# Gate and up projections of a hybrid decoder trunk by seven block products, with the feed-forward units in two parts

## The chip, the cores and the metric

The kernel runs on one core of a Trainium2 chip. The metric is the device time of one launch in microseconds (us). A core has a matrix engine (TensorE, PE in the rows; PEld is its weight load), VectorE (DVE), ScalarE (ACT), GpSimd (POOL) and a queue that issues the DMAs (SP). Each works through its own queue in order and waits for the others by semaphores. SBUF is the working memory, PSUM holds the matrix products in eight banks of 512 float32 a partition.

## The reference

Two layers over 512 tokens of width 1024. Each has a mixer of three sorts of attention heads, a SwiGLU feed-forward of 2816 units, and a gated layer embedding. The change touches the feed-forward alone:

```
h = h + o @ w_out[i]
hn = rms_norm(h, norm_ffn[i])
h = h + (silu(hn @ w_ffn_gate[i]) * (hn @ w_ffn_up[i])) @ w_ffn_down[i]
gate = sigmoid(rms_norm(h, norm_ple[i]) @ w_ple_gate[i])
h = h + (p[i] @ w_ple_proj[i]) * gate
```

All of it is float32 at the interface.

## The kernel before

Every projection is made of three matmuls (`mm3`, L221): both operands are split into a high half, rounded to the matrix engine's float32 format, and a low half, the rest; high x high, high x low and low x high are summed in PSUM. So a weight tile has a path: a DMA into `wraw` (`load_raw`, L192; three buffers of 128x1024, each the rows of four row tiles by 256 columns), ACT copies 512 columns of it into the high half of `whl` (L198), POOL or DVE subtracts that from the raw weights into the low half (L201), and PE loads both halves as weights. `lo_turn` says which of the two: in the feed-forward it is 2, every second low half goes to POOL. There are five `whl` buffers.

`feed_forward` (L1120) first normalizes the rows and transposes them (`norm_T`, L372) into `xT`: activations with the model width on the partitions, in high and low halves, four tiles. Then it goes through 11 blocks of 256 units. Per block, gate and then up: four `whl` tiles each, every tile for 12 matmuls of 512 tokens. A PSUM bank holds 128 units x 512 tokens; a block takes two for gate and two for up. When a block is done, ACT computes Silu from PSUM, DVE multiplies it by up from PSUM, ACT and POOL make the high and low half of `hid`. Block 0 goes first over tokens 0 to 255 and then over the rest, since the later tokens are normalized last. When all 11 blocks are done, the down projection runs over all 22 tiles of units, once for output columns 0 to 511 and once for 512 to 1023, and DVE adds the sums to `h` (L1025).

The order of each engine's queue is set when the program is built, from priorities in the code (`prio`, and `issue_after` for a few) and from what depends on what. `utile` buffers (15 of 128x2048) hold `xT`, `hid`, gains and other large tiles.

Of the kernel before, what the change touches and what calls it, by code (L numbers as in the profile page):

```python
# [10 lines left out]
F32 = mybir.dt.float32  # L11
# [8 lines left out]
P = 128  # L20
S = 512
# [21 lines left out]
def hybrid_trunk_kernel(  # L43
# [47 lines left out]
    def etile(name="e"):  # L91
        return upool.tile([P, 512], F32, name=name, tag="e", bufs=4)
# [97 lines left out]
    turn, lo_turn = [0], [3]  # L190

    def load_raw(view, k, c):  # L192
        raw = wpool.tile([P, 1024], F32, name="wraw", tag="wraw", bufs=3)
        nc.sync.dma_start(raw[:, :k * c].rearrange("p (k c) -> p k c", k=k), view)
        return raw

# [175 lines left out]
    def norm_T():  # L372
# [746 lines left out]

    def feed_forward(i, add_h, between):  # L1120
        lo_turn[0] = 2
        xact = norm_T()
        hidden = []
        for fp in range(NF // 2):
            hid = utile([P, 2, 2, S], name="hid")
            hidden.append(hid)
            tags = "ddss" if fp % 2 == 0 else "stto"
            accs = [bank(t, name=f"gu{j}") for j, t in enumerate(tags)]

            def part(w, a2, ks, cols):  # L1130
                for k, (hi, lo) in ks:
                    for j in range(2):
                        cs = slice(j * P, (j + 1) * P)
                        m = mm3(a2[j][:, cols], hi[:, cs], lo[:, cs], xact(k, 0)[:, cols], xact(k, 1)[:, cols],
                                k == 0 and cols.start == 0, k == KD - 1)
                        if k == 0 and cols.start == 0:
                            first.append(m.ins)

            for wi, w in enumerate((w_ffn_gate[i], w_ffn_up[i])):
                ws = enumerate(weights(w, allk, fp * 256, 256, 2))  # L1140
                first = []
                if fp == 0:

                    ws = list(ws)
                    part(w, accs[2 * wi:2 * wi + 2], ws, slice(0, 256))
                    with tc.issue_after(first[1]):
                        part(w, accs[2 * wi:2 * wi + 2], ws, slice(256, 512))
                else:
                    part(w, accs[2 * wi:2 * wi + 2], ws, slice(0, 512))
            for j in range(2):  # L1150
                sg = etile("sg")
                se.activation(sg, accs[j], AF.Silu)
                ve.tensor_tensor(sg, sg, accs[2 + j], op=ALU.mult)
                se.activation(hid[:, 0, j, :], sg, AF.Copy)
                ge.tensor_tensor(hid[:, 1, j, :], sg, f(hid[:, 0, j, :]), op=ALU.subtract)

        def hact(k, half, tt):
            return hidden[k // 2][:, half, k % 2, tt * P:(tt + 1) * P]

        for c, tags in ((0, "ddss"), (512, "stto")):  # L1160
            if c:
                between()
            else:
                load_gain(norm_ple[i])
            run(project(hact, w_ffn_down[i], list(range(NF)), c, 512, add_h(c), tags=tags, tail=2 if c == 0 else 4))


    def layer_embedding(i):
# [164 lines left out]
```

## Time and profile before

| | |
|---|---|
| median of 3 runs | 1575.32 us (1571.79 to 1575.82) |
| the profiled execution | 1575.22 us, its span 1573.5 us |
| PE busy | 1516.4 us, 96% |
| DVE busy | 746.1 us, 47% |
| ACT busy | 733.1 us, 47% |
| POOL busy | 577.4 us, 37% |
| gate and up, matmuls of 512 columns | 3 x 640, 251 us for each 640 |
| gate and up, matmuls of 256 columns (block 0) | 3 x 128, 36 us for each 128 |

Busy times of one engine can be set side by side along the time axis. Matmuls overlap, so their mean duration is longer than the step from one start to the next; where PE's pace matters, the starts are read. A row of a group gives a mean over the whole kernel, in which undisturbed operations and held ones are mixed; a row of the timeline gives one operation, or several alike in a row (x2) with their time from the first start to the last end.

### The profile page before, as it was taken

Reading aid. Unit: us, or ns where it says so; the run is one execution under the profiler, and the core shown is the slowest. Engines: PE = TensorE matmul, PEld = TensorE weight load, DVE = VectorE, ACT = ScalarE, POOL = GpSimd, SP = SyncE. Lnnn points to the kernel's source line nnn. Section 1 sums busy time; section 2 is a strip of 40 time slices with the busy share of each in tenths; the row PEclk is TensorE's granted clock in tenths of the full one; section 3 lists DMA queues with packets and bytes.
Section 4 is the critical chain, followed back from the end, with each engine's and each line's share of the span. In section 5 each row is a group of like instructions: output and inputs, shape, how many; then the busy total and the mean of one; then the engine's idle time right before and its main releaser. Section 6 shows DMA issues by size and latency. Waiting matters only on the chain.

```text
span 1573.5 us, 23178 instructions
## 1 busy us (share of the span) xinstructions
PE 1516.4 (96%) x8626; PEld 1286.3 (82%) x8626; DVE 746.1 (47%) x1588; ACT 733.1 (47%) x1561; POOL 577.4 (37%) x636
## 2 busy tenths in 40 slices
PE   6999999999999999999999999999999999999997
PEld 6898877879888888888988988778788888888887
DVE  7777869763211111214386878796621111112153
ACT  5467667654333332323355767686433333323243
POOL 4323545453333333321233235465333333323223
PEclk9999999999999999999999999999999999999999
DMA  5411321122333323321224121212133323333221
GB/s 163 136 56 42 82 68 34 48 95 70 97 102 94 94 94 121 119 96 67 81 72 126 49 71 52 80 33 75 55 103 98 94 94 94 100 114 121 94 70 65
DMA packets 114449, 134.58 MB, mean 86 GB/s; under 512 B 6864, under 2 KB 91936, under 8 KB 114336
## 3 DMA queue, kind: packets, MB, share of 16 engines
q1 hardware_dynamic: 114336, 133.10, 27.5%
q8 instruction: 68, 1.11, 0.3%
q14 instruction: 45, 0.37, 0.1%
HBM read 122.59 MB, written 2.10 MB: 79 GB/s over the span
## 4 chain that ended last, share of the span: by engine, by line
PE 73%; DVE 9%; issue 7%; POOL 4%; ACT 4%; DMA 3%; SPq 0%; POOLq 0%; ACTq 0%; DVEq 0%
PE gu L223 10%; PE gu L224 10%; PE gu L222 10%; PE acc L222 6%; PE acc L223 6%; PE acc L224 6%; PE sc L787 2%; PE pTp L808 2%; PE no L1004 2%; PE accr L222 2%; POOL whl L201 2%; PE accr L223 2%; PE accr L224 2%; PE z L698 1%; DMA wraw<-in_w_ple_gate_dram 1%
## 5 line engine op out<-in xcount | busy, mean ns | idle before, releaser
L201 POOL TENSOR_TENSOR whl<-wraw,whl 128x512 fp32r<-128x512 f32 (+2 forms) x248 | 333.7, 1350 | 706.8 <-ACT whl L198 607.6
L198 ACT ACTIVATE whl<-wraw 128x512 fp32r<-128x512 f32 (+2 forms) x416 | 260.6, 631 | 483.0 <-PE gu L224 290.3
L201 DVE TENSOR_TENSOR whl<-wraw,whl 128x512 fp32r<-128x512 f32 x168 | 127.7, 761 | 496.8 <-ACT whl L198 496.1
L224 PE MATMUL gu<-xT,whl 128*128 128x512 f32 (+1 forms) x768 | 287.4, 374 | 0.0
L223 PE MATMUL gu<-xT,whl 128*128 128x512 f32 (+1 forms) x768 | 287.3, 374 | 0.0
L222 PE MATMUL gu<-xT,whl 128*128 128x512 f32 (+1 forms) x768 | 286.8, 373 | 0.0
L223 PEld LDWEIGHTS gu<-xT,whl 128*128 128x128 f32 x768 | 144.2, 188 | 27.5
L224 PEld LDWEIGHTS gu<-xT,whl 128*128 128x128 f32 x768 | 144.2, 188 | 27.4
L222 PEld LDWEIGHTS gu<-xT,whl 128*128 128x128 f32 x768 | 144.4, 188 | 27.1
L223 PE MATMUL acc<-whl,hid 128*128 128x512 f32 x352 | 139.7, 397 | 0.0
L222 PE MATMUL acc<-whl,hid 128*128 128x512 f32 x352 | 139.4, 396 | 0.0
L224 PE MATMUL acc<-whl,hid 128*128 128x512 f32 x352 | 138.8, 394 | 0.0
L800 POOL TENSOR_SCALAR p<-p,rc,gt 128x128 f32<-128x128 f32 (+3 forms) x128 | 79.2, 629 | 71.1 <-DVE rc L798 20.8
L795 ACT ACTIVATE p<-sc,mx 128x128 f32<-128x128 f32 (+3 forms) x160 | 83.9, 536 | 23.0 <-DVE mx L792 21.1
L814 DVE TENSOR_TENSOR pT<-pTp,pT 128x512 fp32r<-128x512 f32 (+2 forms) x120 | 70.6, 595 | 21.2 <-ACT pT L813 20.2
L813 ACT ACTIVATE pT<-pTp 128x512 fp32r<-128x512 f32 (+2 forms) x120 | 62.1, 527 | 38.6 <-PE pTp L808 37.3
L224 PEld LDWEIGHTS acc<-whl,hid 128*128 128x128 f32 x352 | 66.4, 189 | 15.3
L222 PEld LDWEIGHTS acc<-whl,hid 128*128 128x128 f32 x352 | 66.2, 188 | 15.1
L223 PEld LDWEIGHTS acc<-whl,hid 128*128 128x128 f32 x352 | 66.1, 188 | 15.3
L222 PE MATMUL acc<-whl,xT 128*128 128x256 f32 x256 | 74.0, 290 | 1.3 <-DVE rot_b L410 0.6
L792 DVE TENSOR_REDUCE mx<-sc 128x1 f32<-128x384 f32 (+4 forms) x120 | 70.2, 592 | 7.4 <-PE sc L789 7.2
L224 PE MATMUL acc<-whl,xT 128*128 128x256 f32 x256 | 73.3, 288 | 0.0
(298 smaller groups left out, 3320.7 us busy)
## 6 DMA issues: line engine op xcount, KB each, us to landing
wraw<-in_w_ffn_gate_dram SPq DMA_DIRECT2D x44, 512.0 KB, 3.6
wraw<-in_w_ffn_up_dram SPq DMA_DIRECT2D x44, 512.0 KB, 3.6
wraw<-in_w_ffn_down_dram SPq DMA_DIRECT2D x44, 512.0 KB, 3.6
wraw<-in_w_in_dram SPq DMA_DIRECT2D x36, 512.0 KB, 3.5
wraw<-in_w_out_dram SPq DMA_DIRECT2D x16, 512.0 KB, 3.7
wraw<-in_w_ple_gate_dram SPq DMA_DIRECT2D x16, 512.0 KB, 3.5
sw<-nq SPq DMA_DIRECT2D x32, 128.0 KB, 2.3
wraw<-in_w_in_dram SPq DMA_DIRECT2D x8, 280.0 KB, 2.9
```

The costliest lines, as they stand in the source:

```text
L198: se.activation(whl[:, 0], raw[:, lo:lo + n], AF.Copy)
L201: eng.tensor_tensor(whl[:, 1], raw[:, lo:lo + n], f(whl[:, 0]), op=ALU.subtract)
L222: i = te.matmul(acc, lhsT=lh, rhs=rh, start=start, stop=False, skip_group_check=True)
L223: te.matmul(acc, lhsT=lh, rhs=rl, start=False, stop=False, skip_group_check=True)
L224: te.matmul(acc, lhsT=ll, rhs=rh, start=False, stop=stop, skip_group_check=True)
L787: te.matmul(s[:, c:c + w], lhsT=lhsT, rhs=rhs, start=(j == 0), stop=False, skip_group_check=True)
L792: ve.tensor_reduce(mx, sv, axis=AX.X, op=ALU.max, negate=True)
L795: se.activation(e[:, u * n:(u + 1) * n], s[:, u * n:(u + 1) * n], AF.Exp, bias=mx[:, u:u + 1], accum_out=sm[:, u:u + 1])
L800: ge.tensor_scalar(e[:, u * n:(u + 1) * n], e[:, u * n:(u + 1) * n], rc[:, u:u + 1], gates[u] if gates else 1.0, op0=ALU.mult, op1=ALU.mult)
L808: te.transpose(pt[:, kt, :], e[:, kt * P:(kt + 1) * P], ident)
L813: se.activation(hi, src, AF.Copy)
L814: ve.tensor_tensor(lo, src, f(hi), op=ALU.subtract)
```

## The change

The eight plain products of a 2 x 2 split become seven. The weights of a block (1024 rows x 256 units, gate or up) are cut into four pieces of 512 rows x 128 units, `b11` to `b22`; the activations into four pieces, two halves of the model width by two of the tokens. `norm_sums` takes the place of `norm_T` in the feed-forward and makes seven right-hand sides `X1` to `X7`, each 512 rows x 256 tokens in high and low halves: 1, 2 and 4 are pieces as they are, 3, 5, 6 and 7 are sums and differences of pieces (ACT copies `xf`, DVE `s1` to `s4`). `seven` does the same for the weights: three pieces go in as they are, four are differences `T` of 512 columns (T7 = b22 - b12 on POOL; T5 = b12 - b11, T6 = b22 - T5 and T4 = b21 - T6 on DVE). Each of the seven is split into halves in a `whl` tile as before, by ACT and in turn by DVE and POOL, and gives 4 x 3 matmuls of 256 columns. The products are put together behind PE: ACT copies products 1 and 7 and the sum of 1 and 6 out of PSUM, and DVE makes five sums of 256 columns, four with an operand in PSUM and one of two `part` tiles. The sums stand in `gu` tiles in SBUF, so Silu and the product with the gate read SBUF.

Gate and up of a block run one behind the other; in block 0 their products alternate, in an order that begins with those of the first tokens. The raw weights have four buffers for three. The units go in two parts, blocks 0 to 5 and 6 to 10, each with its own down projection, whose sums are added to `h` a part at a time.

```diff
     def load_raw(view, k, c):
-        raw = wpool.tile([P, 1024], F32, name="wraw", tag="wraw", bufs=3)
+        raw = wpool.tile([P, 1024], F32, name="wraw", tag="wraw", bufs=4)
...
+    def norm_sums():
+        g = next_gain.pop()
+        X = Lazy(lambda n: utile([P, 2, 4, 256], name=f"X{n}"))
+        F = {}
+
+        def halve(n, tt, src, eng):
+            hi, lo = (X[n][:, j, :, tt % 2 * P:(tt % 2 + 1) * P] for j in range(2))
+            src = src.rearrange("p (k q) -> p k q", k=4) if len(src.shape) == 2 else src
+            last_act[0] = se.activation(hi, src, AF.Copy)
+            latest["xT"] = eng.tensor_tensor(lo, src, f(hi), op=ALU.subtract)
+
+        with prio(OFN):
+            for tt, kh, xn in normed(g):
...
+                if tt < 2:
+                    halve((1, 2)[kh], tt, pt, ve)
+                    F[kh, tt] = a = etile("xf")
+                    se.activation(a, pf, AF.Copy)
+                elif kh == 0:
+                    F[2] = a = f(sptile("xf"))
+                    se.activation(a, pf, AF.Copy)
+                    s3 = ptile("s3")
+                    ve.tensor_tensor(s3, F[0, tt - 2], a, op=ALU.subtract)
+                    halve(7, tt, s3, ge)
+                else:
+                    s1, s2, s4 = (ptile(n) for n in ("s1", "s2", "s4"))
+                    ve.tensor_tensor(s1, F[2], pf, op=ALU.add)
+                    halve(5, tt, s1, ge)
+                    ve.tensor_tensor(s2, s1, F[0, tt - 2], op=ALU.subtract)
+                    halve(6, tt, s2, ve)
+                    halve(4, tt, pt, ve)
+                    ve.tensor_tensor(s4, F[1, tt - 2], s2, op=ALU.subtract)
+                    halve(3, tt, s4, ge)
+        return X
+
+    def seven(X, w, c0, order, tags, done):
+        raw = [load_raw(w[kh * 512:(kh + 1) * 512, c0:c0 + 256].rearrange("(k p) c -> p k c", p=P), 4, 256)
+               .rearrange("p (k c) -> p k c", k=4) for kh in range(2)]
+        b11, b12, b21, b22 = (raw[i][:, :, j * P:(j + 1) * P] for i in range(2) for j in range(2))
...
+        def combine(n, a, b, eng):
+            T[n] = t = f(swtile("T")).rearrange("p (k c) -> p k c", k=4)
+            eng.tensor_tensor(t, a, b, op=ALU.subtract)
+            return t
+
+        def right(n):
+            if n in (1, 2, 3):
+                return (b11, b21, b22)[n - 1]
+            if n == 7:
+                return combine(7, b22, b12, ge)
+            if n == 5:
+                return combine(5, b12, b11, ve)
+            if n == 6:
+                return combine(6, b22, T[5], ve)
+            return combine(4, b21, T[6], ve)
+
+        out = [ptile(f"gu{j}") for j in range(2)]
+        for n in order:
+            src = right(n)
...
+            se.activation(whl[:, 0], src, AF.Copy)
+            turn[0] += 1
+            (ge if turn[0] % 2 == 0 else ve).tensor_tensor(whl[:, 1], src, f(whl[:, 0]), op=ALU.subtract)
+
+            a = {1: 0, 6: 0, 2: 1, 7: 2, 4: 2, 5: 3, 3: 3}[n]
+            if a not in acc:
+                acc[a] = bank(tags[a], name=f"st{a}")[:, :256]
+            for k in range(4):
+                mm3(acc[a], whl[:, 0, k], whl[:, 1, k], X[n][:, 0, k], X[n][:, 1, k],
+                    k == 0 and n in (1, 2, 7, 5), k == 3 and n in (6, 2, 4, 3))
+            with prio(OFE):
+                if n in (1, 7):
+                    part[n] = eftile("part")
+                    se.activation(part[n], acc[a], AF.Copy)
+                elif n == 5:
+                    part[n] = eftile("part")
+                    ve.tensor_tensor(part[n], part[7], acc[a], op=ALU.add)
+                elif n == 2:
+                    ve.tensor_tensor(out[0][:, :256], part[1], acc[a], op=ALU.add)
+                elif n == 6:
+                    part[n] = eftile("part")
+                    se.activation(part[n], acc[a], AF.Copy)
+                    ve.tensor_tensor(out[1][:, 256:], part[6], part[5], op=ALU.add)
+                elif n == 4:
+                    ve.tensor_tensor(out[0][:, 256:], part[6], acc[a], op=ALU.add)
+                    done(0, out[0])
+                else:
+                    ve.tensor_tensor(out[1][:, :256], part[6], acc[a], op=ALU.add)
+                    done(1, out[1])
+            yield
...
     def feed_forward(i, add_h, between):
         lo_turn[0] = 2
-        xact = norm_T()
...
+        X = norm_sums()
+        hidden, gate = {}, {}
+
+        def gate_done(j, t):
+            gate[j] = t
+            se.activation(t, t, AF.Silu)
+
+        def up_done(j, t):
+            hid = hidden[fp]
+            ve.tensor_tensor(t, t, gate[j], op=ALU.mult)
+            se.activation(hid[:, 0, j, :], t, AF.Copy)
+            ge.tensor_tensor(hid[:, 1, j, :], t, f(hid[:, 0, j, :]), op=ALU.subtract)
...
+        parts = range(0, 6), range(6, NF // 2)
+        for fps in parts:
+            for fp in fps:
+                hidden[fp] = utile([P, 2, 2, S], name="hid")
+
+                order = (1, 2, 7, 5, 6, 4, 3) if fp == 0 else (1, 7, 5, 2, 6, 4, 3)
+                g = seven(X, w_ffn_gate[i], fp * 256, order, "ddss", gate_done)
+                u = seven(X, w_ffn_up[i], fp * 256, order, "sott", up_done)
+                if fp == 0:
+                    for st in (g, g, u, u, *(g, u) * 5):
+                        next(st)
+                run(g, u)
+            end = fps is parts[-1]
+            kts = list(range(2 * fps[0], 2 * fps[-1] + 2))
+            for c, tags in ((0, "ddss"), (512, "stto")):
...
+                run(project(hact, w_ffn_down[i], kts, c, 512, add_h(c, end), tags=tags,
+                            tail=4 if end and c else 2))
```

The order of the instructions shows what this makes of the queues. First DVE in one block of layer 0, in the middle of the stage; `sg` is the gated product of a block before. Before (the whole block):

```order
L1153 TENSOR_TENSOR sg_4732<-sg_4732,gu2_4506 128x512
L1153 TENSOR_TENSOR sg_4737<-sg_4737,gu3_4507 128x512
L201 TENSOR_TENSOR whl_4813<-wraw_4811,whl_4813 128x512
L201 TENSOR_TENSOR whl_4845<-wraw_4843,whl_4845 128x512
L201 TENSOR_TENSOR whl_4892<-wraw_4890,whl_4892 128x512
L201 TENSOR_TENSOR whl_4924<-wraw_4922,whl_4924 128x512
```

And now, less than half of a block; `st` tiles are the products in PSUM, all other names are in SBUF:

```order
L481 TENSOR_TENSOR part_5725<-part_5705,st3_5712 128x256
L483 TENSOR_TENSOR gu0_5667<-part_5685,st1_5730 128x256
L467 TENSOR_TENSOR whl_5826<-T_5824,whl_5826 128x512
L487 TENSOR_TENSOR gu1_5668<-part_5761,part_5725 128x256
L489 TENSOR_TENSOR gu0_5667<-part_5761,st2_5692 128x256
L446 TENSOR_TENSOR T_5986<-wraw_5942 128x512
L467 TENSOR_TENSOR whl_5864<-wraw_5802,whl_5864 128x512
L492 TENSOR_TENSOR gu1_5668<-part_5761,st3_5712 128x256
L446 TENSOR_TENSOR T_6023<-wraw_5944,T_5986 128x512
L467 TENSOR_TENSOR whl_5903<-T_5901,whl_5903 128x512
L446 TENSOR_TENSOR T_6043<-wraw_5944,T_6023 128x512
L481 TENSOR_TENSOR part_5862<-part_5842,st3_5849 128x256
```

Sums that wait for PE (L481 to L492) now stand between the low halves and the differences that PE's next products need.

POOL in one block, before:

```order
L1155 TENSOR_TENSOR hid_4503<-sg_4732,hid_4503 128x512
L1155 TENSOR_TENSOR hid_4503<-sg_4737,hid_4503 128x512
L201 TENSOR_TENSOR whl_4828<-wraw_4811,whl_4828 128x512
L201 TENSOR_TENSOR whl_4860<-wraw_4843,whl_4860 128x512
L201 TENSOR_TENSOR whl_4907<-wraw_4890,whl_4907 128x512
L201 TENSOR_TENSOR whl_4939<-wraw_4922,whl_4939 128x512
```

And now:

```order
L446 TENSOR_TENSOR T_5824<-wraw_5802,wraw_5800 128x512
L467 TENSOR_TENSOR whl_5727<-wraw_5665,whl_5727 128x512
L1234 TENSOR_TENSOR hid_5383<-gu0_5525,hid_5383 128x512
L467 TENSOR_TENSOR whl_5766<-T_5764,whl_5766 128x512
L1234 TENSOR_TENSOR hid_5383<-gu1_5526,hid_5383 128x512
L467 TENSOR_TENSOR whl_5806<-wraw_5800,whl_5806 128x512
L446 TENSOR_TENSOR T_5966<-wraw_5944,wraw_5942 128x512
L467 TENSOR_TENSOR whl_5846<-T_5844,whl_5846 128x512
L467 TENSOR_TENSOR whl_5883<-T_5881,whl_5883 128x512
L467 TENSOR_TENSOR whl_5922<-wraw_5802,whl_5922 128x512
L467 TENSOR_TENSOR whl_5968<-T_5966,whl_5968 128x512
```

Six operations of a block have become eleven.

Last, DVE at the start of the feed-forward, from the norm of token tile 2 on (`xn` is a normalized half row, `xnT` its transpose in PSUM). Before:

```order
L368 SCALAR_TENSOR_TENSOR xn_4462<-h_73,rsr_4457,gx_4325 128x512
L368 SCALAR_TENSOR_TENSOR xn_4471<-h_73,rsr_4457,gx_4325 128x512
L368 SCALAR_TENSOR_TENSOR xn_4485<-h_73,rsr_4480,gx_4325 128x512
L388 TENSOR_TENSOR xT01_4408<-xnT_4464,xT00_4407 128x4x128
L368 SCALAR_TENSOR_TENSOR xn_4494<-h_73,rsr_4480,gx_4325 128x512
L388 TENSOR_TENSOR xT11_4410<-xnT_4473,xT10_4409 128x4x128
```

And now, token tile 2 alone:

```order
L368 SCALAR_TENSOR_TENSOR xn_4468<-h_73,rsr_4463,gx_4325 128x512
L1126 TENSOR_TENSOR h_73<-h_73,acco_4370 128x512
L423 TENSOR_TENSOR s3_4477<-xf_4422,xf_4475 128x512
L368 SCALAR_TENSOR_TENSOR xn_4482<-h_73,rsr_4463,gx_4325 128x512
L467 TENSOR_TENSOR whl_4671<-T_4669,whl_4671 128x512
L446 TENSOR_TENSOR T_4729<-wraw_4590,T_4689 128x512
L427 TENSOR_TENSOR s1_4489<-xf_4475,xnT_4484 128x512
L446 TENSOR_TENSOR T_4749<-wraw_4549,T_4709 128x512
L429 TENSOR_TENSOR s2_4490<-s1_4489,xf_4422 128x512
L446 TENSOR_TENSOR T_4768<-wraw_4590,T_4729 128x512
L432 TENSOR_TENSOR s4_4491<-xf_4434,s2_4490 128x512
L407 TENSOR_TENSOR X6_4497<-s2_4490,X6_4497 128x4x128
```

The sums of the activations and the weight differences of block 0 share the queue; the row tile 3 brings a like set behind it.

## Rows read from the trace of the kernel before

**Rows 1.** the page: busy shares, and TensorE's clock in 40 slices.

```profile
PE 1516.4 (96%) x8626; PEld 1286.3 (82%) x8626; DVE 746.1 (47%) x1588; ACT 733.1 (47%) x1561; POOL 577.4 (37%) x636
...
PEclk9999999999999999999999999999999999999999
```

**Rows 2.** windows, layer 0: block 0, then blocks 1 to 10.

```profile
core 0: us, PE busy (x) PEld busy (x) DVE busy (x) ACT busy (x) POOL busy (x), PEclk, DMA share, GB/s
355.20:382.10 26.90, 26.01 (x215) 25.42 (x214) 10.08 (x16) 11.77 (x22) 7.87 (x9) 1.00 0.19 59
382.10:602.35 220.25, 220.25 (x958) 179.39 (x957) 40.61 (x60) 71.07 (x119) 77.26 (x60) 1.00 0.31 97
```

**Rows 3.** waits from 404 to 600 us: total, times, longest.

```profile
DVE whl L201 <- ACT whl L198: 130.6, 27, 5.3
ACT whl L198 <- PE gu L224: 121.2, 63, 2.2
```

**Rows 4.** timeline of DVE: start, duration, operation; two neighbouring blocks.

```profile
402.75 1.38 DVE L1153 TENSOR_TENSOR sg<-sg,gu 128x512 f32<-128x512 f32 x2 [3.43 <-PE gu L224]
...
424.87 1.38 DVE L1153 TENSOR_TENSOR sg<-sg,gu 128x512 f32<-128x512 f32 x2 [3.43 <-PE gu L224]
```

**Rows 5.** timeline of PE: first product of block 0, block 1, down.

```profile
355.41 0.28 PE L222 MATMUL gu<-xT,whl 128*128 128x256 f32 x1
...
381.10 0.39 PE L222 MATMUL gu<-xT,whl 128*128 128x512 f32 x1
...
602.35 0.40 PE L222 MATMUL acc<-whl,hid 128*128 128x512 f32 x1
```

**Rows 6.** timeline of PE in block 0: first and last of 61.

```profile
364.85 0.28 PE L222 MATMUL gu<-xT,whl 128*128 128x256 f32 x1
...
371.92 0.28 PE L222 MATMUL gu<-xT,whl 128*128 128x256 f32 x1
```

**Rows 7.** groups of ACT: count, busy us, mean ns, idle before.

```profile
L198 ACT ACTIVATE whl<-wraw 128x512 fp32r<-128x512 f32 x400 | 250.1, 630 | 477.3 <-PE gu L224 290.3 <-PE acc L224 139.3 <-PE accT L224 24.0
...
L1154 ACT ACTIVATE hid<-sg 128x512 fp32r<-128x512 f32 x44 | 25.0, 616 | 0.0
```

**Rows 8.** groups of POOL.

```profile
L1155 POOL TENSOR_TENSOR hid<-sg,hid 128x512 fp32r<-128x512 f32 x44 | 56.3, 1302 | 42.1 <-ACT hid L1154 42.1
```

**Rows 9.** groups of DVE.

```profile
L1153 DVE TENSOR_TENSOR sg<-sg,gu 128x512 f32<-128x512 f32 x44 | 30.1, 688 | 70.9 <-PE gu L224 70.9
...
L1237 DVE TENSOR_TENSOR pg<-pg,ge 128x256 f32<-128x256 f32 x32 | 12.7, 417 | 51.2 <-ACT pg L1236 51.2
```

**Rows 10.** timeline of POOL and DVE where they meet, both from SBUF.

```profile
30.42 1.31 POOL L201 TENSOR_TENSOR whl<-wraw,whl 128x512 fp32r<-128x512 f32 x1 [9.01 <-ACT whl L198]
...
31.40 0.88 DVE L201 TENSOR_TENSOR whl<-wraw,whl 128x512 fp32r<-128x512 f32 x1 [1.42 <-ACT whl L198]
...
747.82 3.03 POOL L201 TENSOR_TENSOR whl<-wraw,whl 128x512 fp32r<-128x512 f32 x2 [15.23 <-ACT whl L198]
...
748.52 1.15 DVE L201 TENSOR_TENSOR whl<-wraw,whl 128x512 fp32r<-128x512 f32 x1 [0.82 <-ACT whl L198]
...
750.09 1.04 DVE L1238 TENSOR_TENSOR h<-h,pg 128x256 f32<-128x256 f32 x1
```

**Rows 11.** the same, DVE with an operand in PSUM (acc).

```profile
664.51 0.69 DVE L1025 TENSOR_TENSOR h<-h,acc 128x512 f32<-128x512 f32 x1 [0.69 <-PE acc L224]
664.54 1.32 POOL L201 TENSOR_TENSOR whl<-wraw,whl 128x512 fp32r<-128x512 f32 x1 [0.99 <-ACT whl L198]
```

**Rows 12.** timeline of DVE: the norm of token tile 2.

```profile
357.28 1.42 DVE L368 SCALAR_TENSOR_TENSOR xn<-h,rsr,gx 128x512 f32<-128x512 f32 x2 [0.64 <-POOL rsr L335]
```

More of the change, by code (lines that the diff above doesn't have):

```diff
@@ L393, in norm_T @@
         return act
+    def norm_sums():
[9 more added lines that the diff above has]
+            for tt, kh, xn in normed(g):
+                pt = bank("t", (P, 4, P), name="xnT")
+                for j in range(4):
+                    te.transpose(pt[:, j, :], xn[:, j * P:(j + 1) * P], ident)
+                pf = pt.rearrange("p k q -> p (k q)")
+                if tt < 2:
[18 more added lines that the diff above has]
+        return X
@@ new lines, in seven @@
+    def seven(X, w, c0, order, tags, done):
+        raw = [load_raw(w[kh * 512:(kh + 1) * 512, c0:c0 + 256].rearrange("(k p) c -> p k c", p=P), 4, 256)
+               .rearrange("p (k c) -> p k c", k=4) for kh in range(2)]
+        b11, b12, b21, b22 = (raw[i][:, :, j * P:(j + 1) * P] for i in range(2) for j in range(2))
+        T, acc, part = {}, {}, {}
+        def combine(n, a, b, eng):
[15 more added lines that the diff above has]
+            src = right(n)
+            whl = wpool.tile([P, 2, 560], F32R, name="whl", tag="whl", bufs=5)[:, :, :512] \
+                .rearrange("p t (k c) -> p t k c", k=4)
+            se.activation(whl[:, 0], src, AF.Copy)
[27 more added lines that the diff above has]
+            yield
@@ L1121, in feed_forward @@
         lo_turn[0] = 2
-        xact = norm_T()
[L1123 to L1155, printed above, removed]
@@ L1157, in hact @@
+        X = norm_sums()
[8 more added lines that the diff above has]
+            ge.tensor_tensor(hid[:, 1, j, :], t, f(hid[:, 0, j, :]), op=ALU.subtract)
         def hact(k, half, tt):
             return hidden[k // 2][:, half, k % 2, tt * P:(tt + 1) * P]
[L1160 to L1165, printed above, removed]
+        parts = range(0, 6), range(6, NF // 2)
@@ new lines, in feed_forward @@
+        for fps in parts:
[11 more added lines that the diff above has]
+            for c, tags in ((0, "ddss"), (512, "stto")):
+                if end:
+                    if c:
+                        between()
+                    else:
+                        load_gain(norm_ple[i])
+                run(project(hact, w_ffn_down[i], kts, c, 512, add_h(c, end), tags=tags,
+                            tail=4 if end and c else 2))
```

## The prediction

> **What bounds the kernel now.** I read the shares of the page first: TensorE (PE) is busy 96% of 1573.5 us at a granted clock of 0.9 or more of full speed in every slice [rows 1]. The windows of layer 0's feed-forward say more: in its first block VectorE (DVE) is busy 10.08 of 26.90 us, and in the ten blocks behind it PE is busy the whole 220.25 us while DVE has 40.61 and GpSimd (POOL) 77.26 [rows 2]. The waits of that stretch point the same way: ScalarE (ACT) waits for PE to give back weight buffers, and DVE waits for ACT [rows 3]. So here the three other engines follow PE. The pace can be read twice: the product with the gate starts at 402.75 and again at 424.87 [rows 4], and PE's first full-width product of block 1 starts at 381.10, the down projection at 602.35 [rows 5]: 221.25 / 10 = 22.12 us for a block of 256 units. Block 0, done in token halves, took 381.10 - 355.41 = 25.69 us.
>
> **What it removes.** A block had 96 matmuls of 512 columns: 22.12 / 96 = 0.230 us each. It gets 2 x 7 x 4 x 3 = 168 of 256 columns. The trace has that form in block 0: 60 of them start one after the other from 364.85 to 371.92 [rows 6], 0.1178 us each, every one with its own weight load, as the new ones have. 168 x 0.1178 = 19.79 us. If PE stayed the bound, a block would win 2.33 us.
>
> **What it adds.** Each weight tile now serves 12 matmuls of 256 columns (1.41 us), where it served 12 of 512 (2.76 us). Per block of 256 units (the order rows in the section on the change show it for DVE and POOL):
> - ACT: 14 high halves, 6 copies out of PSUM, 2 Silu, 2 high halves of the result; 24 operations of at most 0.63 us (the whl and hid rows [rows 7]; the PSUM copies are half as wide) = 15.1 us. It fits in 19.79.
> - POOL: 7 low halves, 2 weight differences, 2 low halves of the result: 11 operations, before 6. One took 1.30 us where nothing disturbed it (hid, [rows 8]): 14.3 us.
> - DVE, both operands in SBUF: 7 low halves, 6 weight differences, 2 products with the gate at 0.69 us (sg [rows 9]) and 2 sums of parts at 0.42 (half width, the pg row [rows 9]): 15 x 0.69 + 2 x 0.42 = 11.2 us. Before it had 4 low halves; the product with the gate read PSUM.
> - DVE, one operand in PSUM: 8 sums of 256 columns at 0.42 = 3.4 us.
>
> Each engine alone stays under 19.79. But POOL and the first sort of DVE work don't run at once. In [rows 10] POOL's operation runs from 30.42 to 31.73; DVE's low half starts at 31.40 and ends at 32.28, 0.55 us behind POOL's end. From 747.82 POOL does two in 3.03 us: the first ends at about 749.12, DVE's low half (from 748.52) at 749.67, 0.55 later, and POOL's second at 750.85, 1.18 behind DVE; a half-width DVE sum from SBUF (750.09) then ends at 751.13, 0.28 behind POOL. A DVE sum with a PSUM operand at 664.51 takes its usual 0.69 beside a POOL operation of 1.32 [rows 11]. So the two take turns, and only DVE's work on two SBUF operands is held. Held like this, an operation costs 0.55 (DVE), 0.28 (DVE, half width) or about 1.18 (POOL).
>
> The Trainium skill (SBUF — State Buffer, "SBUF: two separate sides") states such a rule: DVE and GpSimd share a pair of ports as an exclusive lock, also for a DVE operation with two SBUF inputs, held for the whole instruction. The trace agrees on who is held, not on the length: the start-up of the waiting operation is hidden. By the rule's letter the block's turns would add to 14.3 + 11.2 = 25.5 us.
>
> **The sum for a block.** Lower end, turns without a gap: 11 x 1.18 + 15 x 0.55 + 2 x 0.28 = 21.8 us; that alone is over PE's 19.79. Strict alternation of what the queues hold: 11 pairs of 1.18 + 0.55 = 19.0, then 4 x 0.69 + 2 x 0.42 = 3.6, together 22.6. Upper end, all end to end, PSUM sums too: 14.3 + 11.2 + 3.4 = 28.9. The eight PSUM sums mostly stand behind a two-SBUF operation in DVE's queue, so POOL has the turn while they run. But DVE's queue is in order: a sum waits for a PE product, that product for a low half which may be POOL's, and behind the sum stand the next weight differences; and a T buffer (four of them) comes free only when the other engine has done its low half. The five weight buffers cover 7 us, so most of these waits hide. I take an eighth of the way from 22.6 to 28.9, 23.4 us, near the alternation since [rows 10] show it at work. That is 1.3 us slower than 22.12: 20 blocks x 1.3 = +26 us. PE's gain of 2.33 a block is lost, for PE now waits.
>
> **Block 0** (2 x). The seven token sums come out of the same two engines. From DVE's first norm product of token tile 2 (357.28, [rows 12]) to the last low half of block 0, DVE has 21 two-SBUF and 9 PSUM operations and POOL 12 long ones. Turns: 21 x 0.55 + 12 x 1.18 = 25.7 us, up to 383.0; with 0.6 for PSUM sums that don't hide and the last product's 1.41, PE ends it at 385. Its cover is only products 1 and 2 of gate and up, 48 matmuls or 5.6 us. Before it ended at 381.10: +4 us a layer, +8. Bounds: where PE bounds it, block 0 ends 3 to 4 us earlier than now; with every operation end to end (21 x 0.69 + 12 x 1.30 + 9 x 0.5 = 34.6 us) it ends 12 us later.
>
> **Two down passes.** The same matmuls and weight loads (12 + 10 tiles for 22), 8 more DVE sums a layer at 0.69 (the h row [rows 11]) under PE's work; the last block's result is needed by the last of 12 tiles, over 20 us on, so it is covered. At the switch back to gate, five weight tiles can be ready. I take +1 us a layer, +2; between 0 and +4. The fourth weight buffer moves some loads and with them some orders in the mixers, without new work: 0, between -3 and +3.
>
> **Sum.** The profiled execution took 1575.2 us (span 1573.5), the median of the runs is 1575.3: 1575.2 + 26 + 8 + 2 = 1611 us.
>
> **Rivals.**
> - *PE stays the bound* (turns cost less than I read, or the five buffers hide them): -2.33 x 20 = -47, block 0 about -6, +2: 1524 us. For it: today POOL and DVE are mostly idle in these blocks [rows 2]. Against: even turns without a gap need 21.8 us, and the measured holds would have to be a tenth shorter.
> - *The turns are packed without a gap*: 21.8 to 22.2 us a block, PE's gain and the turns cancel: -6 to +2, +6 for the rest: 1575 to 1583 us, at best 1563 where PE bounds block 0. For it: ACT has slack, and alternation needs only that both queues hold ready work. Against: 98% use of one resource by two in-order queues.
> - *Queues block each other*: a DVE sum waiting for PE, behind POOL's low half, keeps weight differences back that POOL's next halves need. Then operations stand end to end: 25.5 to 28.9 us, +68 to +136, and block 0 and the switch +14 to +20: 1657 to 1730 us. It decides when waits take more than 3 us of a block. For it: the DVE rows alternate sums and weights; against: ACT has slack to run ahead, and five weight buffers lie between producers and PE.
> By the skill's rule to the letter the block is 25.5 us and the kernel at 1575.2 + 68 + 14 = 1657, the near end of the last rival.
> - *It doesn't do what it says*: the page would show other than 3696 matmuls of 256 columns; nothing in the order rows speaks for that, no chance of its own.
>
> **Chances.** PE-bound 0.13; packed 0.17 (of it 0.07 faster, 0.05 same, 0.05 slower); forecast 0.47, with its own range 1585 to 1640; blocked queues 0.23. About 0.3% is what a measurement can tell from no change. Faster 0.20, same 0.06, slower 0.74. For 8 in 10 the range goes from 1560, leaving out the PE-bound case, to 1675, into the blocked queues.
>
> **What would show it.** In the changed profile: PE's share falls to about 85 to 90% and in the gate and up stretch it waits for whl tiles of DVE and POOL; DVE's low halves from SBUF average over 1 us for 0.69 undisturbed, while its PSUM sums stay at 0.42; DVE and POOL are both near 75 to 95% busy there; the time between two blocks' gate products is 23 to 24 us; block 0 lasts some 29 us. The forecast is wrong if PE's busy share in that stretch stays at 100% with 19.8 us a block, or if the stretched operations are not those with two SBUF operands. A block of 25 us or more with DVE waiting for PE would show the third rival.

## The result, and the profile after

The changed kernel takes 1687.82 us (median of 4 runs, 1682.48 to 1691.57); the kernel before took 1574.94 (4 runs, 1571.79 to 1575.82). The ratio is 1.0713 [1.0691, 1.0736]: slower by 113 us, where the forecast was 36 us slower and the range ended at 1675. The profiled execution was the fastest of the four; its span is 1680.5 us, 107.0 longer than before.

The page after, shares and TensorE's clock, against [rows 1]:

```profile
PE 1513.7 (90%) x10018; PEld 1347.3 (80%) x10018; DVE 1118.2 (67%) x2038; ACT 852.1 (51%) x1849; POOL 786.5 (47%) x758
...
PEclk9999999999999999999999999999899999999999
```

PE's busy time has hardly fallen (1516.4 to 1513.7) although it computes less: matmuls are more in number, and a busy time of overlapping records isn't a pace. DVE is busy half as long again, POOL a third longer; time in which one is held by the other counts as busy.

The stretches come from PE's starts in layer 0 after, to be read against [rows 5]. The second row is the 169th matmul of its form, with which block 1 begins, since a block has 168; the others are the starts of part 1, its down projection, part 2 and its down projection:

```profile
359.96 0.28 PE L222 MATMUL st<-X,whl 128*128 128x256 f32 x1
...
394.73 0.28 PE L222 MATMUL st<-X,whl 128*128 128x256 f32 x1
...
528.46 0.40 PE L222 MATMUL acc<-whl,hid 128*128 128x512 f32 x1
...
595.05 0.28 PE L222 MATMUL st<-X,whl 128*128 128x256 f32 x1
...
723.28 0.39 PE L222 MATMUL acc<-whl,hid 128*128 128x512 f32 x1
```

The first product of the feed-forward starts 4.55 us later than before (355.41). Block 0 takes 34.8 us, before 25.69 [rows 5], +9.1. The five blocks behind it take 133.7 us, part 2, five blocks, 128.2. Now one steady block, from one weight difference of DVE to the same one a block later:

```profile
412.64 1.75 DVE L446 TENSOR_TENSOR T<-wraw 128x512 f32<-128x512 f32 x1 [4.06 <-POOL whl L467]
...
440.06 1.77 DVE L446 TENSOR_TENSOR T<-wraw 128x512 f32<-128x512 f32 x1 [4.86 <-POOL whl L467]
```

That is 27.42 us, where it was 22.12 [rows 4]. The last block of a part is shorter, so the ten blocks behind block 0 take 133.7 + 128.2 = 262.0 us, before 221.25, +40.7. So a layer loses 4.5 + 9.1 + 40.7 = 54 us, two layers 108, and the span grew by 107: the loss stands in these three places. The windows after (columns as in [rows 2]) are a stretch of block 0 and the steady block:

```profile
367.00:380.00 13.00, 3.80 (x18) 2.92 (x18) 10.10 (x13) 4.44 (x8) 6.75 (x6) 0.69 0.06 20
412.64:440.06 27.42, 22.64 (x168) 21.61 (x168) 20.45 (x25) 11.89 (x24) 16.60 (x12) 0.94 0.24 77
```

The block has the 168 matmuls that were promised. But no engine is full: PE 83%, DVE 75%, POOL 61%. Something makes them wait for each other. The groups of DVE and POOL, against [rows 8, 9]:

```profile
L467 DVE TENSOR_TENSOR whl<-T,whl 128x512 fp32r<-128x512 f32 x88 | 79.3, 902 | 32.5 <-ACT whl L465 32.4
L481 DVE TENSOR_TENSOR part<-part,st 128x256 f32<-128x256 f32 x44 | 18.1, 412 | 4.9 <-PE st L224 4.8
...
L467 POOL TENSOR_TENSOR whl<-wraw,whl 128x512 fp32r<-128x512 f32 x66 | 108.9, 1650 | 96.6 <-ACT whl L465 96.6
L446 POOL TENSOR_TENSOR T<-wraw 128x512 f32<-128x512 f32 x44 | 59.5, 1352 | 122.8 <-DMA wraw<-in_w_ffn_gate_dram 71.6 <-DMA wraw<-in_w_ffn_up_dram 34.8 <-DVE gu L1232 7.5
```

Operations on two SBUF operands are stretched (902 ns for 688, POOL 1650 for 1302), the sum with an operand in PSUM keeps its 412 ns. The last row holds what the prediction doesn't have: before its weight differences POOL stands 106 us, 2.4 for each of the 44, until a DMA of raw weights has landed. The waits from 412 to 640 us, sorted as in [rows 3]:

```profile
POOL whl L467 <- ACT whl L465: 40.0, 13, 4.9
DVE T L446 <- POOL whl L467: 32.5, 12, 4.9
POOL T L446 <- DMA wraw<-in_w_ffn_gate_dram: 21.9, 5, 4.8
...
PE st L222 <- DVE part L481: 12.3, 5, 2.5
```

And how they hang together, in the timeline of one block (DVE first, then the DMA issue, then POOL; rows in between are left out):

```profile
431.50 1.78 DVE L467 TENSOR_TENSOR whl<-wraw,whl 128x512 fp32r<-128x512 f32 x1
433.20 0.41 DVE L481 TENSOR_TENSOR part<-part,st 128x256 f32<-128x256 f32 x1
...
434.80 0.41 DVE L489 TENSOR_TENSOR gu<-part,st 128x256 f32<-128x256 f32 x1
...
433.35 0.37 SPq L194 DMA_DIRECT2D wraw<-in_w_ffn_gate_dram  x1
...
430.98 1.74 POOL L467 TENSOR_TENSOR whl<-wraw,whl 128x512 fp32r<-128x512 f32 x1
437.51 1.29 POOL L446 TENSOR_TENSOR T<-wraw 128x512 f32<-128x512 f32 x1 [4.79 <-DMA wraw<-in_w_ffn_gate_dram]
438.75 2.54 POOL L467 TENSOR_TENSOR whl<-T,whl 128x512 fp32r<-128x512 f32 x2
```

Read it as a ring. DVE's low half of product 3 is the last reader of gate's raw weights; it ends at 433.28. At 433.35 the next gate load goes into that buffer, and it has landed at 437.5. Until then POOL stands 4.8 us at the head of its queue, because the weight difference of the *next* gate half (T_5966 in the order rows of the section on the change) stands there in front of this block's own low halves (whl_5846, whl_5883). DVE's next weight difference waits for those halves to free a T buffer and so stands from 435.2 to 440.06. With four raw buffers, two to each half block, a load can't start before the half block two earlier is done, and by then POOL is already asking for it.

The chain that ended last shows the same ring late in layer 1: DVE's low half, then 4.11 us of DMA, then POOL's difference and low half, then DVE:

```profile
1454.53 1.76 DVE whl L467
1456.33 4.11 DMA wraw<-in_w_ffn_gate_dram
1460.60 1.28 POOL T L446
1461.89 1.25 POOL whl L467
1463.16 1.76 DVE T L446
```

### The profile page after: what moved, and what is told of

It reads as the page before. It is cut to its first block, busy times and chain, and to the rows that moved or that the text cites. A ratio compares the mean times of both kernels' runs of the same rounds, so it can differ in the third digit from the quotient of the medians.

```text
span 1680.5 us, 27128 instructions
## 1 busy us (share of the span) xinstructions
PE 1513.7 (90%) x10018; PEld 1347.3 (80%) x10018; DVE 1118.2 (67%) x2038; ACT 852.1 (51%) x1849; POOL 786.5 (47%) x758
## 3 DMA queue, kind: packets, MB, share of 16 engines
q1 hardware_dynamic: 114336, 133.10, 25.5%
## 5 line engine op out<-in xcount | busy, mean ns | idle before, releaser
L222 PE MATMUL st<-X,whl 128*128 128x256 f32 x1232 | 358.4, 291 | 47.6 <-DVE part L481 41.1
L224 PE MATMUL st<-X,whl 128*128 128x256 f32 x1232 | 361.3, 293 | 41.9 <-POOL whl L467 30.4
L201 POOL TENSOR_TENSOR whl<-wraw,whl 128x512 fp32r<-128x512 f32 (+2 forms) x160 | 219.3, 1377 | 368.0 <-ACT whl L198 347.1
L223 PE MATMUL st<-X,whl 128*128 128x256 f32 x1232 | 355.0, 288 | 0.0
L224 PEld LDWEIGHTS st<-X,whl 128*128 128x128 f32 x1232 | 241.6, 196 | 54.3 <-POOL whl L467 38.7
L222 PEld LDWEIGHTS st<-X,whl 128*128 128x128 f32 x1232 | 241.1, 196 | 52.7 <-issue 44.2
L223 PEld LDWEIGHTS st<-X,whl 128*128 128x128 f32 x1232 | 241.3, 196 | 0.8 <-POOL X L407 0.6
L198 ACT ACTIVATE whl<-wraw 128x512 fp32r<-128x512 f32 (+2 forms) x240 | 149.9, 630 | 180.7 <-PE acc L224 122.4
L467 POOL TENSOR_TENSOR whl<-wraw,whl 128x512 fp32r<-128x512 f32 x66 | 108.9, 1650 | 96.6 <-ACT whl L465 96.6
L467 POOL TENSOR_TENSOR whl<-T,whl 128x512 fp32r<-128x512 f32 x88 | 129.7, 1482 | 28.8 <-ACT whl L465 24.9
L222 PE MATMUL acc<-whl,hid 128*128 128x512 f32 x352 | 139.2, 395 | 0.0
L465 ACT ACTIVATE whl<-T 128x512 fp32r<-128x512 f32 x176 | 109.6, 625 | 35.9 <-PE st L224 27.0
L446 DVE TENSOR_TENSOR T<-wraw,T 128x512 f32<-128x512 f32 x88 | 100.1, 1137 | 25.5 <-POOL whl L467 22.8
L446 POOL TENSOR_TENSOR T<-wraw 128x512 f32<-128x512 f32 x44 | 59.5, 1352 | 122.8 <-DMA wraw<-in_w_ffn_gate_dram 71.6
L467 DVE TENSOR_TENSOR whl<-T,whl 128x512 fp32r<-128x512 f32 x88 | 79.3, 902 | 32.5 <-ACT whl L465 32.4
L896 ACT ACTIVATE p<-sc,mx 128x128 f32<-128x128 f32 (+3 forms) x160 | 83.9, 535 | 22.6 <-DVE mx L893 20.6
```

Source lines behind the costliest of these rows:

```text
L198: se.activation(whl[:, 0], raw[:, lo:lo + n], AF.Copy)
L201: eng.tensor_tensor(whl[:, 1], raw[:, lo:lo + n], f(whl[:, 0]), op=ALU.subtract)
L222: i = te.matmul(acc, lhsT=lh, rhs=rh, start=start, stop=False, skip_group_check=True)
L223: te.matmul(acc, lhsT=lh, rhs=rl, start=False, stop=False, skip_group_check=True)
L224: te.matmul(acc, lhsT=ll, rhs=rh, start=False, stop=stop, skip_group_check=True)
L446: eng.tensor_tensor(t, a, b, op=ALU.subtract)
```

## Experiments

Theory A: the ring of raw buffers makes the blocks longer than the turns of DVE and POOL alone. Theory B: the turns, with DVE's and POOL's work in one chain, are all of it. The short diffs are against the changed kernel where nothing else is said; `...` marks what is left out. Paces are per block of 256 units in the same stretch of layer 0.

**Six raw buffers** (a large tile is given up for the room).

```diff
-        raw = wpool.tile([P, 1024], F32, name="wraw", tag="wraw", bufs=4)
+        raw = wpool.tile([P, 1024], F32, name="wraw", tag="wraw", bufs=6)
-        return upool.tile(list(shape), dt, name=name, tag="u", bufs=15)
+        return upool.tile(list(shape), dt, name=name, tag="u", bufs=14)
```

> The changed kernel with six raw weight buffers for four (and 14 large tiles for 15, which makes room). Theory A, the raw buffers: a buffer comes free only with the last low half of its block, the next load takes 3.7 us, and POOL's weight difference T7 waits for it at the head of POOL's queue; with six, POOL's wait for the DMA (4.8 and 2.2 us a block) goes, and a block falls from 27.4 us to 23 to 24: 1600 to 1620 us. Theory B, turns: POOL and DVE on two SBUF operands exclude each other and that alone makes 27.4 us: the block stays at 27 us, 1685 us.

Measured: 1652.4 us (1646.05 to 1653.13), ratio 1.0466 [1.0441, 1.049]. The pace, from two results of POOL a block apart:

```profile
429.95 1.34 POOL L1234 TENSOR_TENSOR hid<-gu,hid 128x512 fp32r<-128x512 f32 x1 [2.83 <-ACT hid L1233]
438.26 1.40 POOL L446 TENSOR_TENSOR T<-wraw 128x512 f32<-128x512 f32 x1 [1.89 <-DVE whl L467]
...
454.73 1.34 POOL L1234 TENSOR_TENSOR hid<-gu,hid 128x512 fp32r<-128x512 f32 x1 [2.83 <-ACT hid L1233]
```

24.78 us a block. POOL's weight difference no longer waits for a DMA but for DVE. A is right in direction, though its 23 to 24 us and its time were missed; the ring is 2.6 us of the block's 5.3, the rest is something else.

The granted clock is a rival: it was 0.94 in the changed kernel's steady block, 1.00 before. Two neighbouring blocks of this kernel answer it:

```profile
429.95:454.73 24.78, 21.09 (x166) 20.71 (x165) 20.54 (x26) 11.82 (x25) 16.82 (x11) 0.93 0.27 86
454.73:479.50 24.77, 21.02 (x174) 20.46 (x173) 20.49 (x26) 11.64 (x25) 16.82 (x11) 1.00 0.28 86
```

At 0.93 and at 1.00 the block takes the same time. PE follows the other two engines here, and the clock isn't what makes the block long.

**The weights loaded once for each part**, to see whether six buffers take away the whole wait.

```diff
-        raw = [load_raw(...) for kh in range(2)]
+        if key not in kept:
+            kept[key] = [load_raw(...) for kh in range(2)]
+        raw = kept[key]
```

> The weights of gate and up are loaded once in each part of the units, and every block of the part uses those of the first (so the loads of the other blocks are left out). No block waits for a DMA. Theory A: a block takes 22 to 24 us, as with six buffers or a little less. Theory B: 27 us. The kernel's end is not comparable, since the down pass finds its buffers held until the last block; the pace of the blocks is.

Measured: 1644.97 us (one run). The window of one block, and the weight differences of DVE that bound it:

```profile
434.74:459.47 24.73, 20.54 (x161) 19.99 (x161) 20.47 (x25) 11.65 (x24) 16.77 (x11) 0.96 0.01 2
```

```profile
434.74 0.69 DVE L450 TENSOR_TENSOR T<-wraw 128x512 f32<-128x512 f32 x1 [2.44 <-POOL whl L471]
...
459.47 0.69 DVE L450 TENSOR_TENSOR T<-wraw 128x512 f32<-128x512 f32 x1 [2.43 <-POOL whl L471]
```

24.73 us, with 2 GB/s of DMA where there were 77. That is the pace of six buffers, so there the loads cost nothing more; what is left of the block has no DMA in it.

**No low halves of the gate and up weights**: is PE's gain there at all?

```diff
-            turn[0] += 1
-            (ge if turn[0] % 2 == 0 else ve).tensor_tensor(whl[:, 1], src, f(whl[:, 0]), op=ALU.subtract)
-                mm3(acc[a], whl[:, 0, k], whl[:, 1, k], ...
+                mm3(acc[a], whl[:, 0, k], whl[:, 0, k], ...
```

> No low halves of the gate and up weights are made (the third matmul uses the high half again; PE's work is as in the changed kernel): POOL keeps 4 operations a block and DVE loses 7. The port is free for most of the time. This shows what PE alone would take: if 256-column products hold 0.118 us each, a block takes 19.8 to 20.5 us; a wait for raw weights would remain with four buffers and make it 20 to 23.

Measured: 1559.03 us (one run). The window of three blocks, then two results a block apart:

```profile
415.74:475.66 59.92, 59.92 (x506) 59.92 (x505) 36.98 (x55) 37.06 (x73) 18.45 (x12) 1.00 0.35 107
```

```profile
435.39 3.17 POOL L1232 TENSOR_TENSOR hid<-gu,hid 128x512 fp32r<-128x512 f32 x2 [1.29 <-ACT hid L1231]
...
455.69 3.17 POOL L1232 TENSOR_TENSOR hid<-gu,hid 128x512 fp32r<-128x512 f32 x2 [2.35 <-ACT hid L1231]
```

PE is busy the whole stretch. Over the three blocks the pace is 19.97 us, the forecast of 168 x 0.1178 was 19.79. PE's gain is real; in the changed kernel DVE and POOL don't make the weights fast enough for it. POOL's weight differences wait for raw weights here too, 35 us from 412 to 520, but PE waits for nothing in the three blocks: without low halves behind it this wait costs no time. The run also shows what else the change costs: the feed-forward starts at 360.30 (+4.9), part 1 lasts to 493.87, which leaves 133.6 - 5 x 19.97 = 33.7 us for block 0 (+8.0, only 1.1 less than with the low halves), and the ten blocks take 99.9 + 100.2 (part 2) = 200.1 us, -21.2. That is -8.3 a layer, and the span is 16.2 us under that of before. Of the 21.2 us that PE wins in a layer, the start and block 0 take back 12.9.

**POOL's low halves and weight differences on DVE.** POOL keeps only the low half of the result. If the turns are dear, giving DVE more work must make the block shorter.

```diff
-                return combine(7, b22, b12, ge)
+                return combine(7, b22, b12, ve)
-            (ge if turn[0] % 2 == 0 else ve).tensor_tensor(whl[:, 1], src, f(whl[:, 0]), op=ALU.subtract)
+            ve.tensor_tensor(whl[:, 1], src, f(whl[:, 0]), op=ALU.subtract)
```

> All low halves of the gate and up weights and T7 go to DVE; POOL keeps only the two low halves of the result of a block. DVE then has 22 operations on two SBUF operands at 0.69, two at 0.42 and eight PSUM sums at 0.42, 19.4 us a block, and is held only by POOL's two. Theory B: the stretching of DVE's operations goes, a block takes 21 to 23 us, 1570 to 1600 us. Theory A: four raw buffers stay, DVE waits for the DMA in POOL's place, a block takes 25 to 27 us, 1645 to 1690 us.

Measured: 1598.86 us (1597.64 to 1603.19), ratio 1.0143 [1.012, 1.0167]. DVE's groups, the window of three blocks, and in the timeline the pace and a wait:

```profile
L467 DVE TENSOR_TENSOR whl<-T,whl 128x512 fp32r<-128x512 f32 x176 | 120.6, 686 | 13.0 <-ACT whl L465 12.7
...
L467 DVE TENSOR_TENSOR whl<-wraw,whl 128x512 fp32r<-128x512 f32 x132 | 94.2, 715 | 14.2 <-ACT whl L465 13.6
```

```profile
417.36:486.30 68.94, 62.47 (x506) 60.49 (x505) 61.00 (x103) 34.98 (x73) 8.88 (x6) 1.00 0.28 92
```

```profile
436.74 0.69 DVE L446 TENSOR_TENSOR T<-wraw 128x512 f32<-128x512 f32 x1 [1.59 <-DMA wraw<-in_w_ffn_up_dram]
...
440.32 1.34 POOL L1234 TENSOR_TENSOR hid<-gu,hid 128x512 fp32r<-128x512 f32 x1 [18.69 <-ACT hid L1233]
...
463.32 1.34 POOL L1234 TENSOR_TENSOR hid<-gu,hid 128x512 fp32r<-128x512 f32 x1 [18.75 <-ACT hid L1233]
```

23.0 us a block: 4.4 less, though one engine does what two did, and inside theory B's range. The low halves are back near 0.69 us. The expectation's 19.4 us for DVE's work left out the two products with the gate; with them it is 24 x 0.69 + 2 x 0.42 + 8 x 0.42 = 20.8. What is missing is again the wait for raw weights: in the three blocks DVE stands 7.9 us in all, and its six waits for these DMAs, of up to 1.7 us, make 7.7 of them.

**Both, with six raw buffers.** The edits of the first and of the last experiment together.

> Both cures in one: all low halves and T7 on DVE, six raw buffers. Six buffers alone took a block from 27.4 to 24.8 us, DVE alone to 22.9. If the wait for the raw weights and the turns are separate costs, the block falls to 20.5 to 21.5 us (DVE's own operations are 24 x 0.69 + 2 x 0.42 + 8 x 0.42 = 20.8 us), PE-bound would be 19.8: 1550 to 1570 us, under the kernel before. If what is left of alldve is DVE's in-order queue and not the DMA: the block stays at 22.5 to 23, 1595 us.

Measured: 1568.53 us (median of 10 runs, 1565.14 to 1574.07), ratio 0.9964 [0.9946, 0.9981]: faster than both kernels, by 6 us against the one before.

```profile
417.66:480.39 62.73, 60.73 (x511) 60.21 (x511) 61.55 (x103) 35.70 (x73) 8.90 (x7) 1.00 0.32 102
```

```profile
438.57 1.35 POOL L1234 TENSOR_TENSOR hid<-gu,hid 128x512 fp32r<-128x512 f32 x1 [16.65 <-ACT hid L1233]
440.39 1.28 DVE L467 TENSOR_TENSOR whl<-T,whl 128x512 fp32r<-128x512 f32 x2
...
459.48 1.33 POOL L1234 TENSOR_TENSOR hid<-gu,hid 128x512 fp32r<-128x512 f32 x1 [16.64 <-ACT hid L1233]
```

20.91 us a block. Over three blocks DVE is busy 98%, PE 97%: DVE is now the bound, 0.9 us above PE's 19.97. That its work had been put at 20.8 is in part luck: in a row its operations follow each other faster than they last (two in 1.28 us in the middle row, each 0.68, so 0.60 from start to start), and POOL's two operations still hold it in each block. The four kernels make a square:

| us a block | four raw buffers | six |
|---|---|---|
| DVE and POOL in turns | 27.42 | 24.78 |
| DVE alone | 23.0 | 20.91 |

The buffers are worth 2.1 to 2.6 us, one engine in place of two 3.9 to 4.4, nearly independent of each other: two causes, both shown. The second edit takes more than one thing away, as said below.

**The plain products, with the units in two parts** (the kernel before, with only the split of the down projection; the diff is against the kernel before).

```diff
-        for fp in range(NF // 2):
...
+        parts = range(0, 6), range(6, NF // 2)
+        for fps in parts:
+            for fp in fps:
...
+            kts = list(range(2 * fps[0], 2 * fps[-1] + 2))
...
+                run(project(hact, w_ffn_down[i], kts, c, 512, add_h(c, end), tags=tags, tail=4 if end and c else 2))
```

> The kernel before with its plain products and three raw buffers, but the units in two parts with a down projection each. This prices that part of the change alone: I forecast +1 us a layer. Both theories: +1 to +4 us in all, 1576 to 1579 us. If the switch between the passes were what costs, +20 us or more.

Measured: 1576.67 us (10 runs, 1573.68 to 1578.18), ratio 1.000 [0.999, 1.001]. The split costs nothing that can be measured, so the loss is that of the seven products and what came with them. (The fourth raw buffer alone was not run.)

**One large tile fewer, alone** (14 instead of 15), since the six raw buffers were paid for with it.

> The changed kernel with 14 large tiles for 15 and nothing else: the price of the room that six raw buffers need. The mixer of layer 0 ended 5 us later in raw6 than in the changed kernel; if the missing tile does that, the feed-forward starts at about 365 us here too (359.96 in the changed kernel), and the kernel takes some 10 us more, 1698 us; the blocks keep 27.4 us.

Measured: 1695.14 us (one run), 7 us over the changed kernel's median and 4 over its slowest run. The feed-forward starts at 361.12, 1.2 us later than in the changed kernel, and the parts of layer 0 take 2.7 and 3.2 us longer. With six buffers it starts at 365.38, so that start isn't due to the tile alone, which had been expected. The missing tile doesn't make the blocks shorter, so the 2.6 us are the buffers'. One run without an interval doesn't carry more.

**Another order of the products**, in which the raw weights are let go earlier: 1, 5, 7, 2, 3, 6, 4 in place of 1, 7, 5, 2, 6, 4, 3. The sum of products 7 and 5 then stands behind 7. One kernel has it with the change's own engines and buffers, one with DVE alone and six raw buffers.

```diff
-                order = (1, 2, 7, 5, 6, 4, 3) if fp == 0 else (1, 7, 5, 2, 6, 4, 3)
+                order = (1, 2, 7, 5, 6, 4, 3) if fp == 0 else (1, 5, 7, 2, 3, 6, 4)
...
```

> The changed kernel (four raw buffers, POOL and DVE in turn) with that order of products alone. Theory A: the raw weights are free one to two products earlier, so most of the 2.6 us a block that six buffers saved comes back: 25 to 26 us a block, 1640 to 1665 us. Theory B: unchanged, 27.4 us.

> As dve6, with the products of a block in the order 1, 5, 7, 2, 3, 6, 4 (for 1, 7, 5, 2, 6, 4, 3), so that the raw weights are let go two products earlier and the sum of 7 and 5 is awaited two products later than 5. If PE's wait for that sum (L481) is what is left: 0.5 to 1 us a block less than dve6. If DVE's queue is the bound: the same within 0.3%.

Measured: 1703.66 us (one run) with the change's engines, and 1627.25 us, ratio 1.0325 [1.03, 1.035], with DVE alone and six buffers. Both expectations missed. PE's timeline in the first:

```profile
435.78 0.58 PE L222 MATMUL st<-X,whl 128*128 128x256 f32 x1 [4.67 <-DVE part L481]
...
463.95 0.38 PE L222 MATMUL st<-X,whl 128*128 128x256 f32 x1 [4.72 <-DVE part L481]
```

Product 3 adds into the bank that holds product 5, and it may start only when DVE has read that bank for the part sum. In the new order only product 2 stands between the product that completes this sum and product 3, where it was 2, 6 and 4, and PE waits 4.7 us a block for it; in the change's order it waited 2.5 (the row `PE st L222 <- DVE part L481` above). The raw weights do come in time: from 412 to 520 us no wait of POOL for a DMA is left. But this was bought with a worse wait. With DVE alone the same wait is 2.3 us, where it was 0.9, and a block takes 22.7 to 24.2 us.

**The norms of tiles 2 and 3 first**, on top of the kernel with both edits, against the stall in block 0.

```diff
-            for tt, kh, xn in normed(g):
+            items = normed(g)
+            rows = [next(items) for _ in range(4)]
...
+                yield from rows
+                yield from list(items)
...
-                    ve.tensor_tensor(s3, F[0, tt - 2], a, op=ALU.subtract)
+                    ve.tensor_tensor(s3, F[0, tt - 2], pf, op=ALU.subtract)
```

> dve6 with one change at the start of the feed-forward: the norm products of token tiles 2 and 3 stand in DVE's queue before tile 2's sums (in dve6 tile 3's came behind them, and PE stood 9.5 us in block 0), and the sum s3 reads its second operand from PSUM. If PE's stall in block 0 comes from that order, 3 to 5 us a layer go: 1558 to 1563 us, about 0.99 of the kernel before. If DVE is simply full in this stretch, the stall only moves: 1568 us.

Measured: 1568.41 us (12 runs, 1564.32 to 1573.95), ratio 0.9957 [0.9943, 0.9971]: no different from the one without it, as expected for the case that DVE is full there. The largest waits of PE in block 0, first the changed kernel, then the one with both edits, then this:

```profile
374.91 1.09 PE L413 MATMUL xnT<-ident,xn 128*128 128x128 f32 x4 [7.12 <-DVE xn L368]
378.07 0.58 PE L222 MATMUL st<-X,whl 128*128 128x256 f32 x1 [2.07 <-DVE xn L368]
```

```profile
375.92 1.09 PE L413 MATMUL xnT<-ident,xn 128*128 128x128 f32 x4 [6.11 <-DVE xn L368]
```

```profile
373.36 1.09 PE L420 MATMUL xnT<-ident,xn 128*128 128x128 f32 x4 [5.43 <-DVE X L407]
```

The wait for the norm products is gone, and one for the activations' low halves has come: part 1 still takes 136.8 us, 136.0 without. (The feed-forward starts 3.0 us earlier, at 359.33 for 362.35; 2.3 of them are left at the second down projection, 664.83 for 667.17, and none at the start of layer 1's feed-forward, 1134.26 for 1134.09; what takes them there wasn't followed.) In the stalled 13 us DVE is busy 11.75 without this edit and the whole 13.00 with it:

```profile
367.00:380.00 13.00, 4.82 (x33) 4.24 (x32) 11.75 (x16) 5.75 (x11) 6.31 (x6) 0.71 0.06 20
367.00:380.00 13.00, 6.94 (x32) 6.06 (x33) 13.00 (x16) 7.09 (x13) 7.33 (x5) 0.68 0.10 30
```

Block 0 is bound by DVE's work there, with POOL's holds on it, and not by its order.

## Why the prediction was wrong, step by step

- **The removal, 2.33 us a block: right.** Without the low halves PE runs at 19.97 us a block, forecast 19.79.
- **DVE and POOL take turns, and only on two SBUF operands: right.** A held DVE operation takes 1.75 us (the row of 412.64; 1.18 of POOL and 0.55 of its own make 1.73), one of POOL 1.65 in the mean, PSUM sums stay at 0.41. Not every operation is held: in the steady block seven of DVE's last 1.45 us or more. Sharing the work between the two is the larger cause: moving POOL's part to DVE gains 3.9 us a block at six raw buffers. That edit takes away the turns and the handoffs between the two queues at once; which of them has how much of the 3.9 no run tells. For the Trainium skill's rule (SBUF — State Buffer, "SBUF: two separate sides") that means: who is held, the traces confirm. On the length they decide less than the prediction says. A held operation ends 0.55 us behind the other engine's where it lasts 0.69 alone, but DVE's own operations in a row also follow at 0.60, and POOL's at 1.24 (from 438.75 to 439.99 in the timeline row of two). So the 14.3 + 11.2 = 25.5 us, added from durations, may be too long a reading of the rule, and the 24.78 us without a raw wait can't decide between it and the 22.6 of strict alternation, since both engines also wait in that block.
- **"The five weight buffers cover 7 us, so most of these waits hide. I take an eighth of the way": the step that failed.** The steady block is 27.42, three quarters of the way from 22.6 to 28.9. Those five buffers lie behind ACT and the low halves; they hide nothing that stops DVE and POOL themselves. What stopped them were two things. One is in none of the terms: the wait for raw weights, 2.6 us a block. The order rows showed it, T of the next half ahead of this half's low halves in POOL's queue; the prediction counted the raw buffers' number only where it went up (the mixers) and didn't ask when each is let go. A load takes 4.2 us from its issue to POOL's start (433.35 to 437.51), and the buffer is free only with the low half of the last product. The other, 24.78 - 22.6 = 2.2 us, is lost beyond alternation. With six buffers the trace still has two waits in each block: DVE's for POOL's low halves, which free the T buffers (4.1 us), and PE's for the part sum (up to 2.9). Which of them makes the 2.2 no run tells.
- **Block 0, +4 us: too small, inside its bounds.** It is +9.1. The engine was right: PE stands from 367.51 to 378.07 but for four transposes, and waits for DVE's norm product of tile 3, which stands behind tile 2's sums. Putting the norms first only moved the wait, so it is the amount of DVE's work; and as the block is still 33.7 us without the low halves of the weights, these are not the main part of it. What the 5 us were that the sum of turns lacked wasn't taken apart.
- **Two down passes, +1 us a layer: inside its bounds.** The split alone ran at a ratio of 1.000 [0.999, 1.001]: nothing.
- **The mixers, 0 within 3: wrong by 4.5 us a layer.** The feed-forward starts 4.55 us later; with the split alone it starts 0.7 later. The sums of the activations stand among the output projection's sums in DVE's queue, but no run took that apart; it stays open.

The sum with measured terms: ten blocks in 262.0 against 221.25 give +40.7 a layer where the forecast had 10 x 1.3 = +13; twice the difference is 55 of the 71 us by which the span's growth (107) exceeds the forecast's 36. Block 0 adds 10, the mixers 9, and the down passes give 2 back. The third rival's time, 1657 to 1730, held, and the half of its sign that is a block of 25 us or more. The other half, DVE waiting for PE, didn't: from 412 to 520 us DVE's waits are 22.8 us for POOL's low halves and 3.5 for ACT. So its time is right by another mechanism than the one it named: operations do stand behind a waiting one, but the head is a weight difference that waits for a DMA or a T buffer, not a sum that waits for PE. Of the signs of the forecast, POOL's share was missed too (61% in the steady block for 75 to 95). The chances as listed add to 0.05 for the same time and 0.75 for slower, not 0.06 and 0.74.

## What to carry to other kernels

When an edit gives one engine fewer columns and two others more operations, add up first what the two others do in turns, and then follow each buffer through one turn: who reads it last, when the refill is issued, and who stands at a queue's head waiting for it. A queue's order can put the next tile's first operation ahead of this tile's last ones, and then a load that comes late, here by 4.8 us, stops both. Two engines that take turns can be slower than one: here one engine with nearly all the work won 3.9 to 4.4 us a block.

## What the runs showed of the hardware

- TensorE's granted clock was 1.0 in [rows 2]; after, it was 0.94 in the steady block, where PE was busy 83%, and 0.69 from 367 to 380 us, where it stood for 10.6 us but for four transposes. 1.0 is 2.4 GHz and 0.5 would be 1.2 GHz, so these stretches have both levels. PE's products start 0.21 us apart from 380.01 to 381.93, just behind the stand, and 0.118 apart from 382.12 on. With six buffers and DVE alone the clock is 1.00 from 417.66 to 480.39.
- A matmul of 256 columns with a weight load of its own took 0.119 us over three blocks without a pause of PE (59.92 us for 3 x 168), at a granted clock of 1.00.
- One DVE operation after another from SBUF, with little of POOL beside it, kept 686 to 715 ns each in the mean at 88% use (61.00 of 68.94 us). DVE was busy as long in a block when it shared the work with POOL (20.5 us, of which much was held) as when it did nearly all of it (20.5 us too, six raw buffers in both).
